# Feed-forward parts of a two-block kernel: own buffers for modulation blocks, the first two down blocks together, and three small preparations moved into steps

## Chip, cores and metric

One core of a Trainium2 chip runs the whole program. The metric is the time of one execution on the device in microseconds (us). The engines are TensorE (PE in the rows; PEld is its weight load), VectorE (DVE), ScalarE (ACT), GpSimd (POOL) and SyncE (SP), which here only issues transfers. TensorE has two clock levels, 1.2 and 2.4 GHz; a granted clock of 1.00 means the higher one throughout.

## What is computed

The reference chains two blocks over 256 tokens of width 1024. The first block has two layers of attention and feed-forward; the second takes the first's output, modulates it by values that come from a vector `c`, and runs two mixers and a mixture of small experts. Cut to what the change touches:

```python
for i in range(2):                                   # first block
    h = h + heads(rms_norm(h, norm_mix[i])) @ w_out[i]    # attention, i = 0 fox, i = 1 moba
    hn = rms_norm(h, norm_ffn[i])
    gu = hn @ w_gate_up[i]                           # 1024 -> 2 * 2816
    h = h + (silu(gu[..., :2816]) * gu[..., 2816:]) @ w_down[i]
x = rms_norm(h, norm_final)

mod = silu(c) @ w_ada + b_ada                        # second block, 1024 -> 6 * 1024
shift1, scale1, gate1, shift2, scale2, gate2 = split(mod, 6)
h = rms_norm_2(x, norm1_g) * (1 + scale1) + shift1
proj = h @ w_in                                      # latents, lru_x, lru_gate, merge logits
attn = mla_attention(...)                            # uses cos and sin of positions * inv_freq
rec = rg_lru_branch(...)                             # rates: softplus(-lru_lambda)
x = x + gate1 * (mix(attn, rec) @ w_out)
x = x + gate2 * peer_ffn(rms_norm_2(x, norm2_g) * (1 + scale2) + shift2, ...)
```

## The kernel before

All values are float32. A product is formed from three matmuls: each operand is split into a rounded part `hi` and the rest `lo`, and hi x hi, hi x lo and lo x hi are added in PSUM.

**The stream of weights.** A plan lists all weight blocks in the order in which they are used, each of 128 partitions by 1024 columns (512 KB). `Stream.load_to` (lines 183 to 193) issues their transfers on SP into one of four buffers `raw`; `split_to` makes `hi` on ScalarE (line 213) or, for a few blocks of the second block, on GpSimd (line 211), and `lo` on VectorE (line 214). There are four buffers for hi and three for lo, and blocks are split two ahead of use (`AHEAD`). The tile framework orders the instructions of every engine itself, by priority and by its own estimate of times; `issue_after` adds an edge to that order. An engine works off its list in that order.

**The feed-forward part of a layer** has 22 steps of 128 columns. Step f takes a gate and an up block (24 matmuls of 256 columns each, lines 350 to 353), then `gated` multiplies by the row scale `rb` (gu, line 681), applies Silu on ScalarE (684), forms the product (pr, 686) and splits it into `prh` (ScalarE, 338) and `prl` (VectorE, 339). The down block g (12 matmuls of 512 columns, lines 364 to 368) adds the product into four PSUM accumulators; `down_at` (line 58) puts it two steps (`LAG`) behind its gate block, so down 0 follows up block 2. In steps 8 to 15 of layer 0 `mem_chunk` prepares the second layer's memory (`mtl`, line 335).

**The modulation** has 48 blocks of `w_ada`, which are not split: `ada` (line 766) multiplies a block by Silu(c) and sums, in one VectorE instruction (line 774). They lie in the same plan and in the same four raw buffers: one at each feed-forward step of both layers, after that step's up block, and six more in the head projections of layer 1.

**Small preparations.** `csilu` (line 739) loads `c` and applies Silu in layer 0's heads. `prepare_second` (line 832) stands between out-projection and row statistics of layer 0: `angles` (Sin) and `lru_consts` (Abs, Exp and 39 small VectorE operations in both together). The row of the final norm, `gf2`, is loaded and squared at step 2 of layer 1 in program order (lines 707 to 710); the framework issues its load in layer 0's feed-forward part.

**Entry of the second block.** The first blocks of `w_in` (lx) run before the row scale `r` is known: `first_adaln` adds four sums of squares (`ss`) into `s4` on GpSimd (line 958), forms `r` there (lines 288 to 302), and after block lx3 the scale is spread over the partitions by TensorE (line 321). On GpSimd hi casts of lx1, lx4 and lx6 stand in the same list.

## Time and profile before

| | |
|---|---|
| median of 3 runs | 1707.04 us (1702.47 to 1709.91) |
| profiled execution | 1711.15 us, span 1709.3 us, mean granted clock 0.992 |
| TensorE busy in the span | 1675.5 us (98%) |
| VectorE busy | 1215.4 us (71%) |
| ScalarE busy | 875.3 us (51%) |
| GpSimd busy | 298.2 us (17%) |
| moved by transfers | 311.97 MB, 183 GB/s over the span |

The span is the part of the execution that the profile covers. Matmuls overlap each other, so a busy time of one matmul is longer than the distance between two starts. A row of a timeline gives the start in us from the span's start, the duration, the engine, the line in the kernel, the operation with out<-in and the tile's shape, and in brackets how long the engine was idle just before and whose work released it. A row of a table of windows gives, for a stretch, its length, each engine's busy time with the number of instructions, TensorE's granted clock, the busy share of the 16 DMA engines and the rate of the transfers.

### The profile page before, as it was taken

How to read it: one execution, taken by the hardware profiler on the slowest of the kernel's cores; microseconds unless marked ns; L12 is line 12 of the kernel's file. 1: busy time of each engine (PE TensorE's matmuls, PEld its weight loads, DVE VectorE, ACT ScalarE, POOL GpSimd, SP SyncE). 2: the span in 40 equal slices, each digit the busy share in tenths (PEclk: the TensorE clock that was granted, in tenths of full speed). 3: DMA queues.
4: the chain of work that ended last, by engine and by line, in shares of the span. 5: the costliest groups of instructions: out<-in, count | busy, mean ns of one | idle time of the engine just before them, and what ended most of it. 6: DMA issues, size and time to landing. Idle time of an engine off the chain costs nothing.

```text
span 1709.3 us, 30746 instructions
## 1 busy us (share of the span) xinstructions
PE 1675.5 (98%) x11724; PEld 1534.3 (90%) x11724; DVE 1215.4 (71%) x2418; ACT 875.3 (51%) x1500; POOL 298.2 (17%) x396
## 2 busy tenths in 40 slices
PE   8999999999999999999999999999999999999998
PEld 7878998998899998898999999999999888888887
DVE  5767676667676677868777979677888755555555
ACT  5555444455554444689464545444444444444443
POOL 5201000000110003210000010088888300000000
PEclk9999999999999999999999999999999999999999
DMA  6425767765377775453566565644444566666663
GB/s 202 159 87 187 243 231 238 244 210 177 100 242 241 243 240 164 163 185 112 161 209 185 174 184 174 203 145 147 141 144 145 176 186 187 192 187 188 189 188 126
DMA packets 86947, 311.97 MB, mean 183 GB/s; under 512 B 9744, under 2 KB 11024, under 8 KB 86288
## 3 DMA queue, kind: packets, MB, share of 16 engines
q1 hardware_dynamic: 86624, 308.96, 57.2%
q8 instruction: 93, 1.52, 0.4%
q10 hardware_dynamic: 144, 1.05, 0.2%
q14 instruction: 54, 0.44, 0.1%
q0 software_dynamic: 32, 0.00, 0.0%
HBM read 307.87 MB, written 2.10 MB: 181 GB/s over the span
## 4 chain that ended last, share of the span: by engine, by line
PE 52%; DVE 2%; ACT 2%; DMA 1%; issue 0%; POOL 0%; ACTq 0%; DVEq 0%; SPq 0%
PE pb L351 8%; PE pb L350 8%; PE pb L353 8%; PE pa L365 8%; PE pa L364 8%; PE pa L368 7%; PE pa L1543 3%; DVE lo L214 1%; PE pa L353 1%; PE pa L351 0%; PE pa L350 0%; PE pa L1444 0%; DMA raw<-in_w_mg_dram 0%; ACT QT L1149 0%; DMA raw<-in_w_query_dram 0%
## 5 line engine op out<-in xcount | busy, mean ns | idle before, releaser
L214 DVE TENSOR_TENSOR lo<-raw,hi 128x1024 fp32r<-128x1024 f32 (+1 forms) x532 | 649.1, 1221 | 314.0 <-PE pa L368 196.6
L213 ACT ACTIVATE hi<-raw 128x1024 fp32r<-128x1024 f32 (+2 forms) x517 | 541.5, 1050 | 606.6 <-PE pa L365 217.6
L350 PE MATMUL pb<-h1h,hi 128*128 128x256 f32 x1264 | 309.9, 285 | 3.6 <-POOL hi L211 3.0
L351 PE MATMUL pb<-h1l,hi 128*128 128x256 f32 x1264 | 303.8, 280 | 0.6 <-DVE h1l L923 0.6
L1542 POOL TENSOR_SCALAR ring<-iota,slots 128x128 f32<-128x128 f32 x256 | 207.2, 824 | 254.8 <-DVE slots L1509 135.4
L350 PEld LDWEIGHTS pb<-h1h,hi 128*128 128x128 f32 x1264 | 237.6, 188 | 5.1 <-POOL hi L211 3.2
L351 PEld LDWEIGHTS pb<-h1l,hi 128*128 128x128 f32 x1264 | 238.6, 189 | 1.2 <-DVE h1l L923 0.9
L350 PE MATMUL pb<-xth,hi 128*128 128x256 f32 (+1 forms) x936 | 229.4, 284 | 0.0
L351 PE MATMUL pb<-xtl,hi 128*128 128x256 f32 (+1 forms) x936 | 228.1, 282 | 0.0
L364 PE MATMUL pa<-hi,ring_v 128*128 128x512 f32 x512 | 201.9, 395 | 1.1 <-ACT ring_v L338 1.1
L365 PE MATMUL pa<-hi,ring_v 128*128 128x512 f32 x512 | 202.3, 396 | 0.0
L350 PEld LDWEIGHTS pb<-xth,hi 128*128 128x128 f32 (+1 forms) x936 | 178.1, 190 | 6.3 <-issue 2.8
L351 PEld LDWEIGHTS pb<-xtl,hi 128*128 128x128 f32 (+1 forms) x936 | 177.3, 189 | 2.6 <-issue 0.8
L353 PE MATMUL pb<-h1h,lo 128*128 128x256 f32 x1264 | 173.4, 279 | 0.0
L353 PEld LDWEIGHTS pb<-h1h,lo 128*128 128x128 f32 x1264 | 159.0, 188 | 0.0
L368 PE MATMUL pa<-lo,ring_v 128*128 128x512 f32 x512 | 141.1, 396 | 0.0
L353 PE MATMUL pb<-xth,lo 128*128 128x256 f32 (+1 forms) x936 | 129.0, 280 | 4.3 <-DVE lo L214 4.3
L353 PEld LDWEIGHTS pb<-xth,lo 128*128 128x128 f32 (+1 forms) x936 | 117.5, 187 | 5.6 <-DVE lo L214 5.3
L364 PEld LDWEIGHTS pa<-hi,ring_v 128*128 128x128 f32 x512 | 96.2, 188 | 24.3 <-ACT ring_v L338 1.4
L365 PEld LDWEIGHTS pa<-hi,ring_v 128*128 128x128 f32 x512 | 96.1, 188 | 23.6
L368 PEld LDWEIGHTS pa<-lo,ring_v 128*128 128x128 f32 x512 | 96.2, 188 | 23.3
L774 DVE CUSTOM_DVE_ANT_0 raw<-raw,r_rows 128x1024 f32<-128x1024 f32 x48 | 58.7, 1224 | 70.6 <-DMA raw<-in_w_ada_dram 70.5
(431 smaller groups left out, 2476.8 us busy)
## 6 DMA issues: line engine op xcount, KB each, us to landing
raw<-in_expert_u_dram SPq DMA_DIRECT2D x128, 512.0 KB, 3.7
raw<-in_expert_v_dram SPq DMA_DIRECT2D x128, 512.0 KB, 4.3
raw<-in_w_ada_dram SPq DMA_DIRECT2D x48, 512.0 KB, 4.6
raw<-in_w_gate_dram SPq DMA_DIRECT2D x44, 512.0 KB, 3.6
raw<-in_w_up_dram SPq DMA_DIRECT2D x44, 512.0 KB, 4.5
raw<-in_w_down_dram SPq DMA_DIRECT2D x44, 512.0 KB, 4.5
raw<-in_w_out_dram SPq DMA_DIRECT2D x24, 512.0 KB, 3.7
raw<-in_w_mg_dram SPq DMA_DIRECT2D x16, 512.0 KB, 3.4
```

The costliest lines, as they stand in the source:

```text
L213: first = nc.scalar.activation(hi[:, :w], raw[:, :w], AF.Copy)
L214: self.last = first, nc.vector.tensor_tensor(lo[:, :w], raw[:, :w], hi[:, :w], OP.subtract)
L350: mm(p, w[0][:, s], xt[0][:, kc, :], start=kc == 0, stop=False)
L351: mm(p, w[0][:, s], xt[1][:, kc, :], start=False, stop=False)
L353: mm(p, w[1][:, s], xt[0][:, kc, :], start=False, stop=kc == nk - 1)
L364: mm(p, xt[0][:, kc, ts], w[0][:, w0:w0 + n], start=start, stop=False)
L365: mm(p, xt[1][:, kc, ts], w[0][:, w0:w0 + n], start=False, stop=False)
L368: mm(p, xt[0][:, kc, ts], w[1][:, w0:w0 + n], start=False, stop=stop)
L774: nc.vector.tensor_tensor_reduce(out=w, in0=w, in1=self.csb, scale=1.0, scalar=0.0, op0=OP.mult, op1=OP.add, accum_out=self.mod[:, j:j + 1])
L1542: nc.gpsimd.tensor_scalar(ob, iota, slots[:, 1, t:t + 1], None, op0=OP.is_equal)
L1543: nc.tensor.matmul(p[:, j * 128:(j + 1) * 128], oa, ob, start=True, stop=True, skip_group_check=True)
```

## The change

The modulation blocks get two buffers of their own (`ada`), counted apart from the four raw buffers, and may be loaded further ahead in the plan. Downs 0 and 1 both stand at step 3. The pool of the feed-forward part's small tiles is gone; its tiles are slices of tiles under names that the attention part used, with four slots for a product instead of three. `csilu` becomes `load_c`, and its Silu stands after the squares of the row statistics; in layer 1 a Silu of one column stands there. `angles` stands at step 4 of layer 0, `lru_consts` at step 6; the load of `gf2` at step 6 of layer 1 and its Square at step 9. The core of the diff:

```diff
+ADA_BUFS = 2
 def down_at(f):
-    return [NF - 3, NF - 2, NF - 1] if f == NF else [] if f < LAG or f - LAG > NF - 4 else [f - LAG]
+    if f == NF:
+        return [NF - 3, NF - 2, NF - 1]
+    return [0, 1] if f == LAG + 1 else [f - LAG] if LAG + 1 < f < NF - 3 + LAG else []
...
+    def is_ada(self, j):
+        return self.plan[j][0][0] == "ada"
     def load_to(self, n):
...
-            if self.raw and j - min(self.raw) >= RAW_BUFS:
+            ada = self.is_ada(j)
+            if sum(self.is_ada(k) == ada for k in self.raw) >= (ADA_BUFS if ada else RAW_BUFS):
                 return
...
-            t = self.raw_pool.tile([128, 1024], F32, tag="raw", name="raw")
+            if ada:
+                t = self.ada_pool.tile([128, 1024], F32, tag="ada", name="ada")
+            else:
+                t = self.raw_pool.tile([128, 1024], F32, tag="raw", name="raw")
...
-            self.load_to(self.n_split + RAW_BUFS)
+            self.load_to(self.n_split + RAW_BUFS + ADA_BUFS)
...
-                                                   scalar=0.0, op0=OP.add, op1=OP.min, accum_out=mn[:, tt:tt + 1])
+                                                   scalar=3e38, op0=OP.add, op1=OP.min, accum_out=mn[:, tt:tt + 1])
...
-            self.ffn = ctx.enter_context(tc.tile_pool(name="ffn", bufs=2))
+            self.st.ada_pool = ctx.enter_context(tc.tile_pool(name="ada", bufs=ADA_BUFS))
...
-                            self.csilu()
+                            self.load_c()
...
-        dve = los[-1]
-        if i == 0:
-            with self.tc.issue_after(dve.ins), self.tc.issue_after(self.last_hi.ins):
-                self.prepare_second()
         r = self.row_stats()
+        with self.tc.issue_after(self.last_sq.ins):
+            if i == 0:
+                nc.scalar.activation(self.csb, self.csb, AF.Silu)
+            else:
+                warm = self.small.tile([128, 1], F32, tag="warm", name="warm")
+                nc.scalar.activation(warm, self.half[:, 0:1], AF.Silu)
...
+        gus = lay.tile([128, 2, 2, T], F32, tag="qT", name="gus")
+        sgs = lay.tile([128, 4, T], F32, tag="kT", name="sgs")
+        prs = lay.tile([128, 8, 1, T], F32R, tag="hdh", name="prs")
         def gated(f, p):
-            gu = self.ffn.tile([128, 2, T], F32, tag="gu", name="gu")
+            gu = gus[:, f % 2]
...
-            prods[f] = (self.ffn.tile([128, 1, T], F32R, tag="prh", name="prh", bufs=3),
-                        self.ffn.tile([128, 1, T], F32R, tag="prl", name="prl", bufs=3))
+            prods[f] = prs[:, f % 4], prs[:, 4 + f % 4]
...
-            if i and f == 2:
-                self.gf2 = self.load_rows(self.hx, "rows", D, tag="h1h", start=D)
-                nc.scalar.activation(self.gf2, self.gf2, AF.Square)
+            if i and f == 6:
+                with self.tc.issue_after(st.dma.ins):
+                    self.gf2 = self.load_rows(self.hx, "rows", D, tag="h1h", start=D)
+            if i and f == 9:
+                with self.tc.issue_after(st.last[0].ins):
+                    nc.scalar.activation(self.gf2, self.gf2, AF.Square)
+            if i == 0 and f in (4, 6):
+                with self.tc.issue_after(st.last[0].ins), self.tc.issue_after(st.last[1].ins):
+                    self.angles() if f == 4 else self.lru_consts()
```

What this does to the order of instructions is seen at three places. The first is SP's list of transfers at the start of layer 0's feed-forward part (`in_w_gate`, `in_w_up`, `in_w_down` and `in_w_ada` are the four kinds of blocks). Before:

```order
L191 DMA raw<-in_w_gate_dram 128x1024
L191 DMA raw<-in_w_up_dram 128x1024
L191 DMA raw<-in_w_ada_dram 128x1024
L191 DMA raw<-in_w_gate_dram 128x1024
L191 DMA raw<-in_w_up_dram 128x1024
L191 DMA raw<-in_w_ada_dram 128x1024
L191 DMA raw<-in_w_gate_dram 128x1024
L191 DMA raw<-in_w_up_dram 128x1024
L191 DMA raw<-in_w_ada_dram 128x1024
L191 DMA raw<-in_w_down_dram 128x1024
L191 DMA raw<-in_w_gate_dram 128x1024
L191 DMA raw<-in_w_up_dram 128x1024
```

Now:

```order
L201 DMA raw<-in_w_gate_dram 128x1024
L201 DMA raw<-in_w_up_dram 128x1024
L201 DMA raw<-in_w_gate_dram 128x1024
L201 DMA raw<-in_w_up_dram 128x1024
L201 DMA raw<-in_w_gate_dram 128x1024
L201 DMA raw<-in_w_up_dram 128x1024
L201 DMA raw<-in_w_gate_dram 128x1024
L201 DMA raw<-in_w_up_dram 128x1024
L201 DMA ada<-in_w_ada_dram 128x1024
L201 DMA raw<-in_w_down_dram 128x1024 x2
L201 DMA ada<-in_w_ada_dram 128x1024
L201 DMA raw<-in_w_gate_dram 128x1024
```

The ada loads are gone from between the first four gate and up blocks, the first down block is loaded together with the second, one gate and up pair later, and the ada loads come closer together behind that: over the next ten steps there are two or three in a step, where there was one. All 48 are loaded by layer 1's value projection, two of them at the start of the program between its fourth and fifth value block (`in_w_v`); before, the last ones came at layer 1's step 18.

The second place is VectorE's list in the middle of layer 0's feed-forward part, one step from one gu to about the next (line 774 before, 794 after, is the ada product, in two rows; 214 and 224 the lo of a weight block; 335 and 345 the memory's lo). Before:

```order
L681 TENSOR_TENSOR gu<-pb,rb 128x512
L214 TENSOR_TENSOR lo<-raw,hi 128x1024
L686 TENSOR_TENSOR pr<-sg,gu 128x256
L335 SCALAR_TENSOR_TENSOR mtl<-pb,cols,mth 128x256
L214 TENSOR_TENSOR lo<-raw,hi 128x1024
L339 TENSOR_TENSOR prl<-pr,prh 128x256
L774 ISA raw,mod<-raw,r_rows 128x1024
L774 ISA mod 128x1
L214 TENSOR_TENSOR lo<-raw,hi 128x1024
L681 TENSOR_TENSOR gu<-pb,rb 128x512
```

Now:

```order
L698 TENSOR_TENSOR gus<-pb,rb 128x512
L224 TENSOR_TENSOR lo<-raw,hi 128x1024
L702 TENSOR_TENSOR sgs<-sgs,gus 128x256
L345 SCALAR_TENSOR_TENSOR mtl<-pb,cols,mth 128x256
L794 ISA ada,mod<-ada,r_rows 128x1024
L794 ISA mod 128x1
L349 TENSOR_TENSOR prs<-sgs,prs 128x256
L224 TENSOR_TENSOR lo<-raw,hi 128x1024
L794 ISA ada,mod<-ada,r_rows 128x1024
L794 ISA mod 128x1
L224 TENSOR_TENSOR lo<-raw,hi 128x1024
L794 ISA ada,mod<-ada,r_rows 128x1024
```

In the place of one ada product there are three in this step; between the gu of step 3 and that of step 13 there are 25 of them, where there were 10, beside 31 lo.

The third place is GpSimd's list at the entry of the second block (lines 211 and 221 are hi casts of w_in blocks, 958 and 975 the first operation of the chain that makes `r`, and the three rows behind are its next). Before:

```order
L1050 MEMSET r_rows_qk 128x2x32
L1051 TENSOR_SCALAR r_rows_qk<-r_rows_qk 128x96
L211 CAST hi<-raw 128x1024
L958 TENSOR_TENSOR s_7650<-ss_7589 128x4
L960 TENSOR_SCALAR mb<-s_7650 128x2
L961 TENSOR_SCALAR s_7650<-s_7650 128x2
L288 TENSOR_SCALAR ms<-s_7650 128x2
```

Now:

```order
L1067 MEMSET r_rows_qk 128x2x32
L1068 TENSOR_SCALAR r_rows_qk<-r_rows_qk 128x96
L221 CAST hi<-raw 128x1024 x2
L975 TENSOR_TENSOR s_7438<-ss_7377 128x4
L977 TENSOR_SCALAR mb<-s_7438 128x2
L978 TENSOR_SCALAR s_7438<-s_7438 128x2
L298 TENSOR_SCALAR ms<-s_7438 128x2
```

The cast of block lx6 has moved from behind the chain to ahead of it, and follows that of lx4 at once.

TensorE's own list changes little: down 0 and down 1 stand after up block 3 in both layers, where down 0 stood after up block 2, and the second block's order is as before.

## Rows read from the trace of the kernel before

**Rows 1.** The page: busy time, share and instructions of each engine.
```profile
PE 1675.5 (98%) x11724; PEld 1534.3 (90%) x11724; DVE 1215.4 (71%) x2418; ACT 875.3 (51%) x1500; POOL 298.2 (17%) x396
```

**Rows 2.** Windows (length, busy per engine, clock, DMA share, GB/s), layer 0's feed-forward part.
```profile
core 0: us, PE busy (x) PEld busy (x) DVE busy (x) ACT busy (x) POOL busy (x), PEclk, DMA share, GB/s
168.00:176.00 8.00, 6.76 (x32) 5.51 (x33) 6.80 (x19) 4.21 (x8) 0.00 (x0) 0.79 0.42 133
296.00:304.00 8.00, 6.25 (x36) 6.13 (x37) 5.33 (x8) 3.97 (x6) 0.00 (x0) 0.79 0.73 231
200.00:284.00 84.00, 83.98 (x605) 78.60 (x604) 58.40 (x82) 39.52 (x55) 0.00 (x0) 1.00 0.71 240
```

**Rows 3.** Timeline of TensorE: waits in both feed-forward parts, and two starts of downs.
```profile
168.95 0.65 PE L364 MATMUL pa<-hi,prh 128*128 128x512 f32 x1 [2.57 <-ACT prh L338]
...
297.75 1.21 PE L353 MATMUL pb<-xth,lo 128*128 128x256 f32 x8 [2.10 <-DVE lo L214]
...
303.15 0.39 PE L364 MATMUL pa<-hi,prh 128*128 128x512 f32 x1
...
311.54 0.39 PE L364 MATMUL pa<-hi,prh 128*128 128x512 f32 x1
...
317.36 1.20 PE L353 MATMUL pb<-xth,lo 128*128 128x256 f32 x8 [1.01 <-DVE lo L214]
...
494.30 0.97 PE L364 MATMUL pa<-hi,prh 128*128 128x512 f32 x3 [1.50 <-ACT prh L338]
...
626.51 1.20 PE L353 MATMUL pb<-xth,lo 128*128 128x256 f32 x8 [1.14 <-DVE lo L214]
```

**Rows 4.** Timeline of SP's queue and of ScalarE: the final norm's row.
```profile
287.37 0.38 SPq L248 DMA_DIRECT2D r_rows<-in_rows_dram  x1
...
294.06 1.06 ACT L710 ACTIVATE r_rows<-r_rows 128x1024 f32<-128x1024 f32 x1 [3.30 <-DMA r_rows<-in_rows_dram]
```

**Rows 5.** Timeline of VectorE: a small operation, one step, and later ada products.
```profile
170.16 0.16 DVE L883 TENSOR_SCALAR l_s<-l_s 128x8 f32<-128x8 f32 x1
...
284.51 1.23 DVE L774 CUSTOM_DVE_ANT_0 raw<-raw,r_rows 128x1024 f32<-128x1024 f32 x1 [2.02 <-DMA raw<-in_w_ada_dram]
...
285.66 1.22 DVE L214 TENSOR_TENSOR lo<-raw,hi 128x1024 fp32r<-128x1024 f32 x1
286.80 0.68 DVE L681 TENSOR_TENSOR gu<-pb,rb 128x512 f32<-128x512 f32 x1
...
288.53 0.42 DVE L686 TENSOR_TENSOR pr<-sg,gu 128x256 f32<-128x256 f32 x1
288.87 0.48 DVE L335 SCALAR_TENSOR_TENSOR mtl<-pb,cols,mth 128x256 fp32r<-128x256 f32 x1
289.26 1.22 DVE L214 TENSOR_TENSOR lo<-raw,hi 128x1024 fp32r<-128x1024 f32 x1
...
295.33 1.22 DVE L774 CUSTOM_DVE_ANT_0 raw<-raw,r_rows 128x1024 f32<-128x1024 f32 x1 [4.11 <-DMA raw<-in_w_ada_dram]
...
314.93 1.23 DVE L774 CUSTOM_DVE_ANT_0 raw<-raw,r_rows 128x1024 f32<-128x1024 f32 x1 [3.59 <-DMA raw<-in_w_ada_dram]
```

**Rows 6.** Windows, same columns: the two densest longer stretches of transfers.
```profile
3.50:11.50 8.00, 4.16 (x21) 3.62 (x20) 4.56 (x7) 4.61 (x9) 7.86 (x6) 0.83 0.99 332
...
482.00:492.00 10.00, 10.00 (x88) 10.00 (x87) 8.35 (x11) 4.56 (x5) 2.41 (x5) 1.00 0.87 314
```

**Rows 7.** Issues of transfers, 176 to 340 us: count, KB each, median us to landing.
```profile
raw<-in_w_ada_dram SPq DMA_DIRECT2D x18, 512.0 KB, 4.7
```

**Rows 8.** Timeline of ScalarE: a table load.
```profile
165.63 1.28 ACT L684 ACT_TABLE_LOAD   x1
```

**Rows 9.** Timeline of GpSimd at the second block's entry.
```profile
671.66 1.04 POOL L211 CAST hi<-raw 128x1024 fp32r<-128x1024 f32 x1 [8.72 <-PE pa L351]
673.33 1.11 POOL L958 TENSOR_TENSOR s<-ss 128x4 f32<-128x4 f32 x1 [0.64 <-DVE ss L954]
```

**Rows 10.** Timeline of TensorE there: block lx2's lo pass, the spread of r.
```profile
674.74 1.13 PE L353 MATMUL pa<-x1h,lo 128*128 128x258 f32 x8
...
679.85 0.43 PE L321 MATMUL pb<-ident,r 128*128 128x128 f32 x2 [1.10 <-POOL r L302]
```

More of the change, by code (lines that the diff above doesn't have):

```diff
@@ L174, in __init__ @@
         self.split_pool = ctx.enter_context(tc.tile_pool(name="wsplit", bufs=LO_BUFS))
-        self.last = ()
+        self.last, self.ada_pool = (), None
         self.n_loaded = self.n_split = self.n_taken = 0
@@ L280, in sumsq @@
     def sumsq(self, src, dst, junk):
-        self.nc.scalar.activation(junk, src, AF.Square, accum_out=dst)
+        return self.nc.scalar.activation(junk, src, AF.Square, accum_out=dst)
     def rstd(self, ss, n, w):
@@ L531, in row_stats @@
             for tt in range(2):
-                self.sumsq(self.h[:, tt, :], ss[:, tt:tt + 1], self.junk)
+                self.last_sq = self.sumsq(self.h[:, tt, :], ss[:, tt:tt + 1], self.junk)
         return self.rstd(ss, D, 2)
@@ L669, in layer @@
                       lambda kc: los.append(self.norm_chunk(xt2, kc, self.g_ffn, i)), lambda: finish(0))
[L670 to L673 removed]
         r = self.row_stats()
+        with self.tc.issue_after(self.last_sq.ins):
[4 more added lines that the diff above has]
+                nc.scalar.activation(warm, self.half[:, 0:1], AF.Silu)
         acc = [[self.psA(), self.psA()] for _ in range(2)]
         prods = {}
+        gus = lay.tile([128, 2, 2, T], F32, tag="qT", name="gus")
+        sgs = lay.tile([128, 4, T], F32, tag="kT", name="sgs")
+        prs = lay.tile([128, 8, 1, T], F32R, tag="hdh", name="prs")
         def gated(f, p):
[L680 removed]
+            gu = gus[:, f % 2]
             nc.vector.tensor_tensor(gu, p.rearrange("p (a t) -> p a t", a=2),
                                     rb[:, None, :].to_broadcast([128, 2, T]), OP.mult)
[L683 removed]
+            sg, pr = sgs[:, f % 2], sgs[:, 2 + f % 2]
             nc.scalar.activation(sg, gu[:, 0, :], AF.Silu)
[L685 removed]
             nc.vector.tensor_tensor(pr, sg, gu[:, 1, :], OP.mult)
[L687 to L688 removed]
+            prods[f] = prs[:, f % 4], prs[:, 4 + f % 4]
             self.split((prods[f][0][:, 0, :], prods[f][1][:, 0, :]), pr)
@@ L737, in layer, with load_c @@
         return xt
-    def csilu(self):
+    def load_c(self):
         self.csb = self.load_rows(self.hx, "rows", D, tag="h1l")
-        self.nc.scalar.activation(self.csb, self.csb, AF.Silu)
     def out_proj(self, key, x, order, evict, after, between=None):
@@ L830, in gate_rows @@
             self.nc.vector.tensor_copy(t[:, k * 512:(k + 1) * 512], p)
-    def prepare_second(self):
-        self.angles()
-        self.lru_consts()
     def angles(self):
```

2 lines of the change are left out of this document (removed).

## Prediction

> **What bounds the kernel now.** I read the page first, then the windows, then TensorE's timeline at its waits, then the other engines around each wait. The page names TensorE: busy 1675.5 of 1709.3 us, VectorE 1215.4, ScalarE 875.3 [rows 1]. So only what leaves TensorE waiting, or slows its clock, is worth anything. The windows sort the stretches [rows 2]: from 200 to 284 us, ten steps of layer 0's feed-forward, TensorE is busy for 83.98 of 84 us at the full clock (2.4 GHz), while VectorE has 25.6 us and ScalarE 44 us free. A step there takes 311.54 - 303.15 = 8.39 us from one down block to the next [rows 3]. This stretch cannot get shorter; it can only get longer. What can get shorter are the holes at its edges. TensorE waits 2.57 us for the first down block's product (ScalarE's prh), 2.10 and 1.01 us for a lo half late in layer 0, 1.50 us for layer 1's first product, and 1.14 us for a lo half at the end of layer 1's feed-forward [rows 3]. After the two longest, the granted clock is 0.79 on average over 8 us [rows 2]: part of the stretch ran at 1.2 GHz, which costs 8 x 0.21 = 1.7 us each time.
>
> **The sum's base.** The rows come from one execution of 1711.15 us (span 1709.3, 1.85 around it). The median of the three runs is 4.1 us lower. I sum against 1711.15 and then take off 4.1.
>
> **Removed: waits.**
> (a) Layer 0's first down block. Today it stands after the third up block, and prh comes 2.57 us late. Moved one step, downs 0 and 1 stand after the fourth up block: two blocks of 24 matmuls, 5.6 us (the step less its twelve wide matmuls, 8.39 - 2.8), lie in between, more than the 2.57 us. Products 0 and 1 now have to live longer, which their four slots allow. Gain 2.6 + 1.7 = 4.3.
> (d) Likewise layer 1's first down block: 1.5. It had no visible drop of the clock behind it.
> (b) The wait at 297.75. The final norm's row is issued on SP at 287.37, ahead of an ada load, lands 6.7 us later, and its Square on ScalarE starts at 294.06 after 3.30 us of waiting [rows 4]. All hi casts stand behind that Square; at the same time VectorE waits 4.11 us for the ada block [rows 5]. The change puts load and Square into steps 6 and 9 of layer 1. Gain 2.1 + 1.7 = 3.8. In its new place ScalarE has the 6.7 us of landing covered by three steps of 8.39, so I cost it at nothing; without that cover it would be 3.3 again.
> (c) The lo waits at 317.36 and 626.51 come behind an ada product that itself waits for its load (3.59 us of VectorE idle ahead of the first) [rows 5]. In the changed order no ada stands at either place. Gain 1.0 + 1.1 = 2.1.
> Sum of the gains: 11.7. It cannot be more than these holes hold, since nothing in the change shortens matmuls.
>
> **Added: (f) the dense stretch.** The ada blocks no longer take their turn in the four raw buffers, one per step. Their two own buffers let the planner load them ahead: 25 stand between the gated products of steps 3 and 13, not 10. VectorE's bill for these ten steps, by pitch on its timeline [rows 5]: 25 ada and 31 lo at 1.15 us (284.51 to 285.66) 64.4; ten each of gu 0.68, pr 0.34 and prl taken as pr, 13.6; five mtl at 0.39, 2.0; 39 small operations of angles and rates at about 0.1, 3.9. Together 83.9 of the 84 us that ten steps take. So VectorE, with 30% free today, has nothing left for waits, and it executes in order: an ada product that waits for its load holds up the lo behind it, and TensorE needs that. The transfers: 55 blocks of 0.524 MB, 28.8 MB in 84 us, or 343 GB/s. Today's stretch has 240 [rows 2]. The densest stretches of the trace are 332 GB/s over 8 us at the start, with the engines 0.99 busy, and 314 over 10 us in layer 1 [rows 6]. At 320 GB/s, 28.8 MB take 90 us: +6. Bounds: zero, if the queue holds 343 when it is kept full; +18, from the loop of the two ada buffers. That loop is landing 4.7 us [rows 7], product 1.15, turn-round some 0.9: 6.8 us for two blocks, so 25 take 85 us, just level; with a landing of 6 us, nearer to the 6.7 of [rows 4], they take 100, +16, and 2 more for the clock. I take +6, since today's landings of 4.7 us are from a stretch at 70% of that load.
> The Trainium skill, "DMA: Bandwidth & Descriptors", section Specifications, gives about 358 GB/s of HBM bandwidth for each NeuronCore. By it 28.8 MB would take 80 us, the DMA would not bound this stretch, and the sum would be 6 us less. No window of 8 us or more in this trace comes to that figure.
>
> **Moved, at little or nothing.** Angles and rates leave the place before the row statistics, from where their small operations on VectorE reach in among the first gated products (170.16) [rows 5]; their 3.9 us are in (f). On ScalarE the change has 23 table loads for 24, of 1.28 us [rows 8]; two now lie in steps 6 and 7, behind 44 us of free time over ten steps, so nothing; uncovered they would be 2.6. The new start of the min reduction changes no duration.
> (h) Start: two ada loads (1.05 MB) go between the fourth and fifth value block, while the queue is 0.99 busy [rows 6]. At 332 GB/s they are 3.2 us of transfer, mostly behind matmuls that run until then: +0.5, bounds 0 to 3.
> (i) The five last ada loads stand between layer 1's value loads: +0.5, bounds 0 to 4.
>
> **(g) Entry of the second block.** On POOL the cast for block lx6 now stands ahead of the chain that makes r. Today that chain starts at 673.33, right behind lx4's cast at 671.66 [rows 9]. The cast for lx6 needs the hi buffer of block lx2, which TensorE gives back when its hi pass ends, at 674.74 [rows 10]: cast from 674.9 to 675.95, chain some 2.6 us later. TensorE waits 1.10 us for r now [rows 10], so it would wait 3.7, which is longer than the waits that were followed by half clock; with 1.7 for that it makes +4 (bounds 0, if the cast finds its buffer early, and +7).
>
> **Sum:** -11.7 + 6 + 4 + 0.5 + 0.5 = -0.7: 1710.4 against 1711.15; 4.1 lower, **1706 us**. What the holes give, the dense stretch and the entry take back.
>
> **Rivals.**
> (B) The dense stretch is covered. Transfers hold 343 GB/s, ada blocks sit in their buffers before VectorE comes, and the loss in (f) is 0 to 3; the entry costs 2. For it: a queue with more issues waiting is fuller, and landing covers turn-round. Against it: no window shows that rate for long. Time: -11.7 + 2 + 2 + 1 is -7, down to -12: 1695 to 1700, middle 1697. The page's bandwidth figure above would make this the case.
> (C) Slower: the ada loop. When two blocks take longer than 6.7 us from load to load (2.5 blocks in 8.39 us), each ada product makes VectorE wait, the lo halves queue behind it, and TensorE stands at each. The deciding point is a landing of about 4.7 us in the stretch. At 6 us it is +16, with the clock +18: 1706 + 12 = 1718, and up to 1722 with the entry's upper bound. For it: VectorE waits at ada products already now, up to 4.11 us [rows 5], with landings at 4.7; the r_rows load took 6.7. Against it: these waits are today's late issue behind other raw buffers, which the own buffers end.
> (D) The change does not end the first wait: three ada products now stand ahead of the row scale rb, the third waits for its load, and products 0 and 1 come that much later. (a) is lost: about 1710.
>
> **How the numbers follow.** 0.5%, 8.5 us, is about what a measurement of this kernel can tell from no change: 1698.5 to 1715.6. Forecast (between -8 and +8) 0.50; B 0.27, nearly all beyond -8.5 if (f) is nothing; C 0.18; D 0.05, some of it slower if the waits add up. Faster 0.28, same 0.50, slower 0.22. The range goes from all gains at the lowest costs, 1695, less 2 for the spread of the runs, to C's 1718 and 1 more: 1693 to 1719. The likeliest case alone: 1699 to 1713.
>
> **What would show it.** (a), (b), (c), (d) right: no TensorE idle over 1 us before the first down block of either layer, and none behind an ada product at the end of layers 0 and 1. (f) right: VectorE 95% busy between steps 3 and 13, transfers at 320 GB/s, and ten steps in 90 us, with TensorE's idle released by lo; at 84 us B holds, at 100 us with VectorE waiting for ada loads C holds. (g) right: TensorE's wait for r at the entry at 3 to 4 us with a lower clock behind it. The prediction is wrong if the dense stretch costs under 2 or over 12 us.

## Result and profile after

The changed kernel takes 1719.36 us (median of 6 runs, 1716.38 to 1721.59), the kernel before 1707.21 in the same set: a ratio of 1.0072, 95% interval 1.0056 to 1.0088. It is slower by 12 us, where 1706 us and no change had been forecast, and it lies just above the forecast range of 1693 to 1719 us.

The page of the changed kernel has the same matmuls and almost the same work on every engine; TensorE is busy 9 us longer than in [rows 1].

```profile
PE 1684.8 (98%) x11724; PEld 1542.4 (90%) x11724; DVE 1220.1 (71%) x2418; ACT 875.9 (51%) x1500; POOL 291.6 (17%) x396
```

Since TensorE's order is nearly the same, the same matmul can be found in two traces, and the difference of its two starts says where time is gained or lost. This table gives by how many us that difference grew in each stretch (limits in the time of the kernel before; every trace is set against the profiled execution of the kernel before, which ended 4 us above its median). The lower rows belong to experiments told below.

| kernel | to 102 | 102-127 | 127-202 | 202-285 | 285-327 | 327-654 | 654-690 | 690-815 | 815-1353 | sum |
|---|---|---|---|---|---|---|---|---|---|---|
| changed | -1.3 | +1.8 | -4.4 | +7.8 | -4.9 | -3.4 | +4.9 | +4.3 | +5.5 | +10.3 |
| before_shift | -1.1 | 0.0 | -0.8 | +0.5 | -1.2 | -1.7 | +0.3 | +1.2 | +6.3 | +3.4 |
| before_shift64 | -2.3 | 0.0 | +0.2 | +1.1 | -3.3 | +0.4 | +0.1 | +2.1 | +9.1 | +8.5 (1.2 behind 1353) |
| before_shift256 | -2.2 | 0.0 | +1.1 | -0.3 | 0.0 | -0.9 | +0.1 | +0.6 | +0.1 | -1.6 |
| after_noshift | -1.3 | +1.8 | -4.8 | +2.8 | -5.4 | -2.0 | +5.6 | -0.4 | +0.1 | -3.7 |
| after_held | -1.9 | +1.9 | -4.2 | +0.5 | -4.9 | -3.1 | +6.2 | -1.2 | +5.3 | -1.3 |
| after_sums | -1.5 | +3.4 | -4.3 | +4.7 | -4.9 | -0.6 | +1.4 | +4.8 | +6.2 | +9.1 |
| noshift_first_downs | -1.0 | +1.8 | -4.1 | +5.4 | -5.3 | -1.3 | +5.5 | +4.6 | -1.0 | +4.5 |
| held_noshift | -1.7 | +1.8 | -4.8 | -0.3 | -5.3 | -3.7 | +6.1 | -1.6 | -1.6 | -10.9 |
| held_noshift_sums | -0.2 | +1.8 | -4.8 | -0.3 | -5.3 | -4.5 | +1.4 | +0.2 | -0.1 | -11.9 |
| repaired_shared | -1.4 | +1.8 | -4.8 | +3.2 | -3.5 | +0.1 | +1.4 | +0.1 | -1.3 | -4.4 |
| repaired_all_three_back | -1.4 | 0.0 | -3.8 | -0.3 | -5.3 | -4.2 | +1.4 | +0.5 | -0.2 | -13.4 |
| three_back_shared | -1.6 | 0.0 | -3.3 | +2.7 | -4.0 | +3.7 | +1.5 | +0.3 | -0.8 | -1.6 |

The three before_shift kernels have the kernel before's order of instructions. What they gain or lose in a stretch whose work is the same shows how far two executions differ: about 2 us at the start and 3 us around 300. So the traces say where, and the times how much. Their waits differ too: ahead of layer 0's first down block TensorE waits 2.52, 1.86 and 3.33 us in them (2.57 in the kernel before), for the lo behind the final norm's row 2.07, 0.60 and 3.04 us (2.10 before), and the waits of 1.01 and 1.14 us that the forecast counted as (c) occur in none of them at these lengths.

The forecast gains are all there: 127-202 (first down block), 285-327 (final norm's row) and part of 327-654. What outweighs them stands in four places, and there is a smaller one in layer 0's attention (102-127).

**Layer 0's dense stretch.** Windows of the changed kernel, columns as in [rows 2]; the first runs from the gu of step 3 to that of step 13:

```profile
174.74:272.45 97.71, 95.27 (x668) 87.94 (x666) 83.67 (x155) 45.25 (x64) 0.00 (x0) 1.00 0.88 309
200.00:284.00 84.00, 79.53 (x546) 72.91 (x545) 70.62 (x129) 38.56 (x53) 0.00 (x0) 0.98 0.87 301
...
270.00:284.00 14.00, 11.97 (x76) 10.87 (x76) 11.55 (x19) 7.25 (x11) 0.00 (x0) 0.88 0.72 246
```

Where TensorE was busy 83.98 of 84 us (200 to 284), it now has 79.53, and the clock falls behind the longest wait. The timelines of TensorE (all its waits in this stretch) and of VectorE (two of its long waits at an ada product):

```profile
209.18 1.21 PE L363 MATMUL pb<-xth,lo 128*128 128x256 f32 x8 [0.73 <-DVE lo L224]
...
244.31 1.21 PE L363 MATMUL pb<-xth,lo 128*128 128x256 f32 x8 [0.48 <-DVE lo L224]
...
254.33 1.21 PE L363 MATMUL pb<-xth,lo 128*128 128x256 f32 x8 [0.71 <-DVE lo L224]
...
260.90 1.22 PE L363 MATMUL pb<-xth,lo 128*128 128x256 f32 x8 [0.47 <-DVE lo L224]
...
274.71 1.21 PE L363 MATMUL pb<-xth,lo 128*128 128x256 f32 x8 [2.02 <-DVE lo L224]
```

```profile
241.29 1.22 DVE L794 CUSTOM_DVE_ANT_0 ada<-ada,r_rows 128x1024 f32<-128x1024 f32 x1 [2.24 <-DMA ada<-in_w_ada_dram]
...
271.30 1.23 DVE L794 CUSTOM_DVE_ANT_0 ada<-ada,r_rows 128x1024 f32<-128x1024 f32 x1 [4.25 <-DMA ada<-in_w_ada_dram]
```

The lo that TensorE waits for at 274.71 stands on VectorE behind the ada product that waited 4.25 us until 271.30. The chain of the forecast is there, 4.4 us of it as waits. The loads issued from 260.9 to 267.2, around the longest wait, took 6.4 to 7.3 us to land; the median over the whole stretch is 4.9. The size varies from one execution to the next: the three other traces with products crowded like this (after_noshift, after_sums, noshift_first_downs) lost 2.8, 4.7 and 5.4 us here, and not 7.8.

**Entry of the second block.** Timelines of TensorE, GpSimd and VectorE, and as the last VectorE's last sum in the kernel before:

```profile
679.11 0.69 PE L331 MATMUL pb<-ident,r 128*128 128x128 f32 x2 [4.81 <-POOL r L312]
```

```profile
670.60 1.07 POOL L221 CAST hi<-raw 128x1024 fp32r<-128x1024 f32 x1 [2.97 <-PE pa L361]
673.44 1.11 POOL L975 TENSOR_TENSOR s<-ss 128x4 f32<-128x4 f32 x1 [1.77 <-DVE ss L971]
```

```profile
672.67 0.68 DVE L971 CUSTOM_DVE_ANT_0 junk<-sq,r_rows 128x512 f32<-128x512 f32 x1
```

```profile
671.73 1.51 DVE L954 CUSTOM_DVE_ANT_0 junk<-sq,r_rows 128x512 f32<-128x512 f32 x1 [0.37 <-ACT sq L282]
```

TensorE waits 4.81 us for r, not 1.10 as in [rows 10]. But the cast of lx6 ended at 671.67; GpSimd then waited 1.77 us more for the last of the four sums, which VectorE made from 672.67 to 673.35. The chain starts as late in absolute time as in [rows 9], although all before it had come 4 us earlier. The cause, tested below, is VectorE's order: before, the framework had put the first sum (662.55) and the second (667.12) among the splits of the token chunks, and now all four stand behind them, the first at 666.68. From 680 to 690 us the granted clock is 0.90, where it was 1.00.

**Matmuls that are each a little slower.** From 815 to 1353 us TensorE waits no longer than before (it is busy for 535.96 of these 538 us, and was for 534.94), its clock is 1.00 in both kernels, and yet 5.5 us go. The window from 1110 to 1310 us, in the kernel before and in the changed one:

```profile
1110.00:1310.00 200.00, 200.00 (x1736) 200.00 (x1735) 166.15 (x410) 90.24 (x211) 175.99 (x216) 1.00 0.48 145
```

```profile
1110.00:1310.00 200.00, 200.00 (x1714) 200.00 (x1713) 160.49 (x391) 89.39 (x205) 167.68 (x205) 1.00 0.47 144
```

In 200 us TensorE gets through 1714 matmuls instead of 1736, 1.3% fewer. By the distance from one start to the next, the median over the same rows, the matmuls that read h1l (the lo half of the transposed tokens) take 119 ns and not 117.

**A wait at 787.78** of 2.47 us for VectorE, which with the lower clock behind it (0.77 from 785 to 800) makes most of the 4.3 us in 690-815. VectorE was late because a row of the final norm, issued at 765.78, arrived at 772.49:

```profile
787.78 2.07 PE L393 MATMUL pa<-QT,QT 96*128 96x128 f32 x6 [2.47 <-DVE mn L409]
```

The column 690-815 shows such a loss in some executions and not in others of the same order (-0.4 in after_noshift), so the order alone does not bring it. Three of the four traces with crowded products have it, and of the other changed kernels repaired_gf2 (+4.6) and in part held_noshift_sums_csilu (+2.5); whether the crowding makes it more frequent is not shown.

### The profile page after: what moved, and what is told of

Same layout as the page of the kernel before. It is cut to its first block, busy times and chain, and to the rows that moved or that the text cites. A ratio compares the mean times of both kernels' runs of the same rounds, so it can differ in the third digit from the quotient of the medians.

```text
span 1719.6 us, 30784 instructions
## 1 busy us (share of the span) xinstructions
PE 1684.8 (98%) x11724; PEld 1542.4 (90%) x11724; DVE 1220.1 (71%) x2418; ACT 875.9 (51%) x1500; POOL 291.6 (17%) x396
## 4 chain that ended last, share of the span: by engine, by line
PE 53%; DVE 3%; DMA 1%; ACT 1%; issue 0%; POOL 0%; DVEq 0%; ACTq 0%; SPq 0%
PE pb L360 8%; PE pb L361 8%; PE pb L363 8%; PE pa L375 8%; PE pa L378 7%; PE pa L374 7%; PE pa L1560 3%; DVE lo L224 1%; PE pa L363 1%; PE pa L361 0%; PE pa L360 0%; PE pa L1461 0%; DMA r_rows<-in_rows_dram 0%; DMA raw<-in_w_query_dram 0%; DVE rr L1334 0%
## 5 line engine op out<-in xcount | busy, mean ns | idle before, releaser
L360 PE MATMUL pb<-h1h,hi 128*128 128x256 f32 x1264 | 314.0, 287 | 2.6 <-POOL hi L221 2.0
L361 PE MATMUL pb<-h1l,hi 128*128 128x256 f32 x1264 | 307.9, 282 | 0.8 <-DVE h1l L940 0.8
L794 DVE CUSTOM_DVE_ANT_0 ada<-ada,r_rows 128x1024 f32<-128x1024 f32 x48 | 58.6, 1222 | 30.0 <-DMA ada<-in_w_ada_dram 28.8
```

The lines of the kernel that those rows point to most:

```text
L360: mm(p, w[0][:, s], xt[0][:, kc, :], start=kc == 0, stop=False)
L361: mm(p, w[0][:, s], xt[1][:, kc, :], start=False, stop=False)
L794: nc.vector.tensor_tensor_reduce(out=w, in0=w, in1=self.csb, scale=1.0, scalar=0.0, op0=OP.mult, op1=OP.add, accum_out=self.mod[:, j:j + 1])
```

## Experiments

Ratios are to the kernel before, timed in the same set of runs.

**The position of the tiles.** The one-column Silu of layer 1 got a tile of its own, `warm`, with four slots of 32 bytes in the pool of small tiles. All tiles allocated behind it (token rows, transposed tokens, the experts' tiles) lie 128 bytes higher in each partition; the weights' buffers do not move. *before_shift* puts an unused tile there in the kernel before:

```diff
         r = self.row_stats()
+        if i:
+            self.small.tile([128, 1], F32, tag="warm", name="warm")
```

> The kernel before, with one unused column tile of four slots in the pool of small tiles: its 128 bytes per partition push every later tile (token rows, transposed tokens, the experts' tiles) up by 128 bytes, as the change's one-column Silu tile does. The order of instructions is the same on all engines. Theory 1 (the position of the tiles makes the matmuls slower): matmuls between 880 and 1350 us stretch by 0.15 to 0.35 us in 20 us and in layer 1's feed-forward part by 0.15, 6 us in all: 1713. Theory 2 (that stretching belongs to the one profiled execution or to something else in the change): no difference, 1707 within 2.

Measured: 1715.76 against 1704.72, 1.0058 (1.0035 to 1.0081). *after_noshift* takes the tile out of the change:

```diff
-                warm = self.small.tile([128, 1], F32, tag="warm", name="warm")
-                nc.scalar.activation(warm, self.half[:, 0:1], AF.Silu)
+                warm = self.small.tile([128, 2], F32, tag="inv", name="inv")
+                nc.scalar.activation(warm[:, 0:1], self.half[:, 0:1], AF.Silu)
```

> The changed kernel with the one-column Silu writing into an existing slot of the small tiles (tag inv) and not into a tile of its own, so that all later tiles lie where they lay before the change; the order of instructions is the same. Theory 1: the 6 us of slow stretching go, 1713. Theory 2: no difference, 1719 within 2.

Measured: 1709.12, 1.0025 (1.0013 to 1.0037). Both agree with theory 1, with more than its 6 us, and exclude theory 2: the same order of instructions, and 128 bytes cost some 10 us in the one kernel and 8 us (1.0072 less 1.0025, of 1707) in the other. The matmuls account for it: over all that start within 0.3 us of the one before them in both traces, the distances between starts add up to 10.0 us more in before_shift than in the kernel before (8.9 of them behind 500 us, 6.4 between 815 and 1353), and to 9.1 us more in the changed kernel than in after_noshift. The window of 1110 to 1310 us, before_shift, then after_noshift:

```profile
1110.00:1310.00 200.00, 200.00 (x1713) 200.00 (x1713) 163.20 (x401) 89.73 (x209) 173.27 (x213) 1.00 0.46 143
```

```profile
1110.00:1310.00 200.00, 200.00 (x1735) 200.00 (x1734) 166.45 (x411) 90.16 (x212) 176.40 (x217) 1.00 0.47 144
```

*before_shift256* and *before_shift64* are the same edit with 256 and 64 bytes:

```diff
+            self.small.tile([128, 16], F32, tag="warm", name="warm")
...
+            self.small.tile([128, 1], F32, tag="warm", name="warm", bufs=2)
```

> The kernel before with the later tiles pushed up by 256 bytes and not 128; same order of instructions. If the matmuls' extra time depends on where a tile lies within 256 bytes, it is gone: 1705, and matmuls that read h1l take 116.0 ns on average between 1110 and 1310 us. If any place other than the old one is slow, or if the slowness has a longer period: 1710 to 1716 and 118 to 119 ns.

Measured: 1707.23 against 1705.35, 1.0014 (1.0000 to 1.0029): the loss is gone, or nearly.

> The kernel before with the later tiles pushed up by 64 bytes; same order of instructions. Where the tile of transposed tokens begins, modulo 256, is 64 in the kernel before (fast), 192 with 128 bytes (slow) and 64 with 256 bytes (fast); here it is 128. If only what lies 128 off is slow: 1705. If any start other than 64 is slow: 1710 to 1716, with matmuls that read h1l at 118 to 119 ns and not at 116.

Measured: 1720.92 against 1705.45, 1.0083 (1.0066 to 1.0099): 64 bytes cost most, more than the 1716 expected at the highest; the median distance at h1l is 123 ns. The same window, 256 bytes, then 64:

```profile
1110.00:1310.00 200.00, 200.00 (x1735) 200.00 (x1734) 166.54 (x412) 89.83 (x210) 176.54 (x218) 1.00 0.46 143
```

```profile
1110.00:1310.00 200.00, 200.00 (x1701) 200.00 (x1701) 161.66 (x395) 89.01 (x206) 170.21 (x209) 1.00 0.46 143
```

**The crowding of modulation products.** *after_held*:

```diff
-            self.ada(1, f == 0)
+            self.ada(1, True)
```

> The changed kernel with each modulation product held behind its step's lo split, one per step as before, still in two buffers of its own. Theory of the ada loop: the 7.8 us that layer 0's steps 3 to 13 lost against the kernel before go, with the gains at the first downs kept: 1711 to 1712, ten steps in 84 us. Rival (what slowed these steps is the rate of transfers or the two small preparations, not the crowding of ada products): at most 3 us are gained, 1716 or more.

Measured: 1711.98, 1.0053 (1.0036 to 1.0070). The stretch 202-285 loses 0.5 us instead of 7.8. Its window, and its ada loads (number, KB, median us to landing):

```profile
200.00:284.00 84.00, 84.00 (x596) 78.52 (x595) 64.77 (x114) 43.24 (x59) 0.00 (x0) 1.00 0.77 245
```

```profile
ada<-in_w_ada_dram SPq DMA_DIRECT2D x10, 512.0 KB, 4.5
```

TensorE is busy throughout, with the same two buffers: in this stretch it is the crowding that costs. The whole time gains less than the stretch: the kernel before was 2.5 us faster in this set, and 1.0072 less 1.0053 is 0.19% or 3 us, within the intervals and at the limit of what the rival allowed. Without the shift the gain is clear: held_noshift (below) has 0.9975 where after_noshift has 1.0025, 0.50% or 8.5 us. Between these two traces the dense stretch gives 3.1 us of 7.2; the rest is spread over the columns behind 327.

**The order of the sums.** *after_sums* writes the loop of the sums into the loop over the halves, so that VectorE's list has the first two sums ahead of the second half's splits:

```diff
             late()
-        for nh in range(2):
-            c = slice(nh * 512, (nh + 1) * 512)
             for tt in range(2):
                 k = 2 * tt + nh
```

> The changed kernel with the sums of squares at the second block's entry written behind each half of the chunks and not behind both, so that on VectorE the first two sums come before the second half's splits and GpSimd's chain for r stands before the cast of lx6. Theory (TensorE's wait for r at the entry, some 5 us with the clock, is the order of these sums): 1714. Rival (the chain starts when TensorE gets there, whatever the order): 1719 within 2.

Measured: 1715.71, 1.0060 (1.0043 to 1.0078). The stretch 654-690 loses 1.4 us and not 4.9. The time alone, 0.12% less than the changed kernel's and within the intervals, does not settle it. *held_noshift* leaves only this repair out of the kernel with all three:

> The kernel with two of the three repairs: one product per step and no shift, the sums in the order of the change. Theory: the entry of the second block is 4 us longer than in the kernel with three repairs (5.5 against 1.5 us lost there), so 1701. Rival (the entry's wait is hidden in most executions): 1698 or less.

Measured: 1700.23, 0.9975 (0.9962 to 0.9989), 654-690 at +6.1. *held_noshift_sums* has all three repairs:

> The changed kernel with three repairs at once: one modulation product per step, the one-column Silu in an existing slot (no shift), and the sums of squares behind each half. If the three losses are separate and add (5 for the crowding, 8 for the shift, 3 to 4 for the sums, from 1717 on the chip that gave 1704.7 for the kernel before): 1700, which is 0.2 to 0.4% faster than the kernel before. Rival (they share a wait, or something else of the change costs as much): 1705 or more.

Measured: 1696.98 against 1705.35, 0.9951 (0.9935 to 0.9966). The sums are worth 0.24%, 4 us, and the repaired change is faster than the kernel before by 0.5%. Whether the three losses add is not shown: all repairs together gain 1.21% (21 us) over the changed kernel, each alone 0.47, 0.19 and 0.12% (13 us in all), and the intervals are too wide to tell these apart. Nor was the kernel before run with its sums in the new order; but the repaired kernel still loses 1.4 us against it in 654-690, so its gain does not lie there. TensorE and GpSimd at the entry, in held_noshift_sums:

```profile
667.81 0.43 PE L331 MATMUL pb<-ident,r 128*128 128x128 f32 x2 [1.09 <-POOL r L312]
```

```profile
661.89 0.20 POOL L973 TENSOR_TENSOR s<-ss 128x4 f32<-128x4 f32 x1 [1.77 <-DVE ss L969]
...
668.10 1.04 POOL L221 CAST hi<-raw 128x1024 fp32r<-128x1024 f32 x1
```

The wait for r is back at its old length, 1.09 us.

**Which part brought which gain.** *noshift_first_downs* is after_noshift with the old `down_at`:

```diff
-    return [0, 1] if f == LAG + 1 else [f - LAG] if LAG + 1 < f < NF - 3 + LAG else []
+    return [] if f < LAG or f - LAG > NF - 4 else [f - LAG]
```

> The changed kernel without the shift (1709.1), and with the first two down blocks again at steps 2 and 3. Theory: TensorE's waits ahead of the first down block return in both layers with their lower clock, 4.3 and 1.5 us: 1715. Rival (the product is in time anyway in the new order of VectorE): 1709 within 2.

Measured: 1707.59, 1.0022 (1.0004 to 1.0041), not slower than after_noshift; TensorE waits 0.39 us at layer 0's first down block and not at all at layer 1's. A miss of the theory. From here on one part is put back into held_noshift_sums. *repaired_downs* (old `down_at`):

> The kernel with three repairs, and the first two down blocks again at steps 2 and 3. From the earlier run with the old place: a wait of at most 0.5 us in layer 0 and none in layer 1, so 1697 to 1697.7. Rival (with one ada product per step VectorE's order brings the wait back): 1699 to 1701.

Measured: 1698.23, 0.9966 (0.9954 to 0.9978). *repaired_prep*:

```diff
+        if i == 0:
+            with self.tc.issue_after(los[-1].ins), self.tc.issue_after(self.last_hi.ins):
+                self.angles()
+                self.lru_consts()
         r = self.row_stats()
...
-            if i == 0 and f in (4, 6):
-                with self.tc.issue_after(st.last[0].ins), self.tc.issue_after(st.last[1].ins):
-                    self.angles() if f == 4 else self.lru_consts()
```

> The kernel with three repairs (1697.0), and angles and rates again before layer 0's row statistics. The run with the old place of the first downs still had no wait there, so another part must have removed it. Theory: it was these preparations, whose small VectorE operations stood among the first gated products: TensorE again waits about 2.5 us for the first down block of layer 0, with the clock 4.5 us: 1701. Rival (two causes, each enough: the later downs cover what the preparations delay): no wait over 0.5 us, 1697.

Measured: 1697.23, 0.9958 (0.9945 to 0.9972), no wait at the first down block. *repaired_gf2*:

```diff
-            if i and f == 6:
-                with self.tc.issue_after(st.dma.ins):
-                    self.gf2 = self.load_rows(self.hx, "rows", D, tag="h1h", start=D)
-            if i and f == 9:
-                with self.tc.issue_after(st.last[0].ins):
-                    nc.scalar.activation(self.gf2, self.gf2, AF.Square)
+            if i and f == 2:
+                self.gf2 = self.load_rows(self.hx, "rows", D, tag="h1h", start=D)
+                nc.scalar.activation(self.gf2, self.gf2, AF.Square)
```

> The kernel with three repairs, and the final norm's row loaded and squared at step 2 of layer 1 in program order, which puts both into layer 0's feed-forward part again (order differs in these two instructions alone). Theory: TensorE's wait of 2.1 us for a lo half behind ScalarE's wait for this row comes back, with the clock 3.8 to 4.4 us: 1701. Rival (that wait came from the ada load behind it on SP, which own buffers have taken away): 1697 within 1.5.

Measured: 1698.21, 0.9964 (0.9952 to 0.9976). The rival: 285-327 keeps its whole gain, -5.3, though ScalarE's Square waits 3.18 us for the row, about as long as in [rows 4]. *repaired_shared* (the modulation blocks in the raw buffers again):

```diff
-            if sum(self.is_ada(k) == ada for k in self.raw) >= (ADA_BUFS if ada else RAW_BUFS):
+            if self.raw and j - min(self.raw) >= RAW_BUFS:
...
-            if ada:
-                t = self.ada_pool.tile([128, 1024], F32, tag="ada", name="ada")
-            else:
-                t = self.raw_pool.tile([128, 1024], F32, tag="raw", name="raw")
+            t = self.raw_pool.tile([128, 1024], F32, tag="raw", name="raw")
...
-            self.load_to(self.n_split + RAW_BUFS + ADA_BUFS)
+            self.load_to(self.n_split + RAW_BUFS)
```

> The kernel with three repairs, but with the modulation blocks in the four raw buffers again. Theory (own buffers bring something: an ada load no longer stands ahead of the gate and up loads for the same buffers, and the lo waits of 1.0 and 1.1 us late in layer 0 and at the end of layer 1 go): these waits come back, 1699 to 1700. Rival (held to one per step, own buffers are worth nothing): 1697 within 1.

Measured: 1705.71, 1.0011 (0.9998 to 1.0024). The theory held in kind, with a larger size: held to one product per step, own buffers are worth 0.6% of 1707, 10 us (0.45 to 0.53% against the three kernels of its own set), 3.5 of them in the stretch 202-285 of the trace and 4.6 in 327-654. But the two named waits did not come back: TensorE now waits for hi casts, 1.10 us at 218.81, 0.86 at 290.50 and 1.96 at 335.40. The 2.10 us for a lo half stay away too, with the row moved and without own buffers. *held_noshift_sums_csilu*:

```diff
                             self.load_c()
+                            nc.scalar.activation(self.csb, self.csb, AF.Silu)
...
-            if i == 0:
-                nc.scalar.activation(self.csb, self.csb, AF.Silu)
-            else:
+            if i:
```

> The three repairs, and Silu of c again right behind its load in layer 0's heads, as before the change. All traces of the changed kernel show layer 0's attention between 105 and 120 us 1.8 to 2 us longer than before. If the place of this Silu (its tables, and with it ScalarE's order there) is the cause, that stretch gets 1.8 us shorter and the run as much against the kernel with three repairs; and the first gated product of layer 0 may pay a table load again. Rival (the order there comes from the two early modulation loads): the stretch stays as long.

Measured: 1696.27, 0.9951 (0.9936 to 0.9966). The stretch 102-127 loses nothing now instead of 1.8 us, in this trace and in the three others with that Silu in the heads; the time shows no difference from held_noshift_sums. It is the lowest median of all in us, but not clear of its neighbours.

The wait ahead of the first down block took four more runs, all on held_noshift_sums. *repaired_prep_downs* (the edits of repaired_prep and repaired_downs):

> The kernel with three repairs, with angles and rates again before the row statistics and the first two downs again at steps 2 and 3. Each alone brought no wait back. If these two are the causes, each enough: TensorE waits 2 to 3 us for layer 0's first down block, 1700 to 1701. If it is the Silu table, which stands ahead of the first gated product only where Silu of c is not behind the squares: no wait over 0.5 us, 1698.

Measured: 1699.62, 0.9968 (0.9953 to 0.9984), no wait. *repaired_csilu_downs* (those of held_noshift_sums_csilu and repaired_downs):

> The kernel with three repairs, Silu of c in layer 0's heads again (so the Silu table is loaded right ahead of the first gated product) and the first two downs again at steps 2 and 3; angles and rates stay inside the steps. If the table load alone makes the first product late: a wait of about 1.3 us or more ahead of the first down block. If it takes the preparations: none over 0.5 us.

Measured: 1697.62, 0.9951 (0.9932 to 0.9969), a wait of 0.31 us. *repaired_all_three_back* (all three, and no one-column Silu):

> The kernel with three repairs, and all three back: downs at steps 2 and 3, angles and rates before the row statistics, Silu of c in the heads and none behind the squares in either layer. Every theory of this wait expects it here: 2 to 3 us ahead of layer 0's first down block, 1.5 us ahead of layer 1's; 1702. If it is absent, the wait belonged to the ada loads in the raw buffers or to the old slots of the products.

Measured: 1697.76, 0.9944 (0.9925 to 0.9963), no wait. So none of the three. What is left first are own buffers, and ScalarE's timeline says how. The cast ahead of the Silu, in the kernel before and in repaired_all_three_back:

```profile
164.55 1.06 ACT L213 ACTIVATE hi<-raw 128x1024 fp32r<-128x1024 f32 x1 [1.57 <-DMA raw<-in_w_gate_dram]
```

```profile
161.60 1.06 ACT L221 ACTIVATE hi<-raw 128x1024 fp32r<-128x1024 f32 x1 [2.32 <-PE pb L359]
162.68 1.28 ACT L698 ACT_TABLE_LOAD   x1
163.97 0.42 ACT L698 ACTIVATE sgs<-gus 128x256 f32<-128x256 f32 x1
```

Before, the first Silu (166.93) stood behind a cast that waited for a gate block, whose load SP issued at 158.56, behind those of a modulation block (155.96) and a down block (157.25). With own buffers that block is there, and the Silu runs 3 us earlier, table load and all; 1.4 of them are this execution's head start (column to 102). *three_back_shared* adds the edit of repaired_shared:

> The run with all three parts back, and with the modulation blocks in the four raw buffers again. In the trace of the kernel before, ScalarE's Silu for the first product stands behind a hi cast that waits for a gate block until 164.55 us, and that load waits for a buffer behind two modulation blocks. Theory (own buffers alone end the wait, moved downs alone too): here neither is there, so TensorE waits 2 to 3 us ahead of layer 0's first down block, and the run takes 1705 to 1708. Rival (one product per step or the new slots of the products ended it): no wait over 0.5 us.

Measured: 1703.04, 0.9982 (0.9969 to 0.9994); waits of 0.77 and 0.20 us at layer 0's first down block, less than expected. At layer 1's the wait is back in full: 1.85 us for prh (here `prs`, L342) and 0.56 for prl, where repaired_all_three_back has none and the kernel before 1.50 [rows 3]. TensorE, then ScalarE:

```profile
489.60 0.73 PE L368 MATMUL pa<-hi,prs 128*128 128x512 f32 x2 [1.85 <-ACT prs L342]
```

```profile
488.19 1.06 ACT L217 ACTIVATE hi<-raw 128x1024 fp32r<-128x1024 f32 x1 [1.68 <-DMA raw<-in_w_gate_dram]
489.15 0.71 ACT L342 ACTIVATE prs<-sgs 128x256 fp32r<-128x256 f32 x2
```

A cast that waits for a gate block stands ahead of the product's cast. So a late gate block in front of ScalarE does bring this wait, and the buffers alone end it: nothing else differs between these two kernels. With own buffers the wait stays away whichever part is put back; in shared buffers it stays away with the other parts of the change in place (repaired_shared, -4.8), so those parts together are enough too; which of them is not shown. In layer 0, with neither, 1.0 us came back and not 2.5, and the gate block was not late there. What made up the rest in the kernel before stays open.

## Why the prediction was wrong

By its own steps:

- **What failed: "nothing in the change shortens matmuls", taken for "changes", and the part "moved, at little or nothing".** The one-column Silu was looked at for its table load alone. Its tile moved everything behind it by 128 bytes, and matmuls, most of them behind 500 us, became up to 1.3% slower: 8 us, shown by two pairs of kernels with the same order of instructions. No term and no rival had it. Without it the result is 1.0025, 4 us slower, inside the range and on the side of no change; the 5 us that still separate it from the forecast's 1 us faster are not traced to one place.
- **(a), (d), first downs: right in size, wrong in cause.** Forecast 4.3 and 1.5; the stretch 127-202 gained 4.4 to 4.8. But with the old place of the downs the gain stayed: with own buffers the move has nothing left to gain. The row named the releaser (prh), and I stopped there; the Silu behind a cast behind a late gate block was two steps further back on ScalarE. The 1.7 us for the clock are not sure either: behind the wait of 2.52 us in before_shift the granted clock stays at 1.00 from 160 to 182 us.
- **(b), (c): right in size for one execution, wrong in part of the cause.** Forecast 3.8 and 1.0 in this stretch; 4.9 to 5.4 came, against an execution that had both waits. With the row's load back at its old step the gain came all the same, so with own buffers the move is not needed; with the move and shared buffers 3.5 us of it stayed (repaired_shared). The waits of (c) are not in the three other traces with the order before, so its 2.1 us are largely a matter of that one execution.
- **(f), the dense stretch: about right in size, by luck; wrong in mechanism.** Forecast +6 from the rate of transfers; four traces show +2.8 to +7.8. VectorE's bill was right, 83.67 us busy against 83.9, but it is not a full engine: the ten steps take 97.71 us, where those steps took 88.89 before, so that it is 86% busy and not 95%. The transfers run at 309 GB/s and not 320. What costs is waits in order: loads that take 4.9 us at the median, and 6.4 to 7.3 around the longest wait, behind an issue that waits for a buffer. This is rival C's mechanism at the forecast's price. In C's loop the turn-round of 0.9 us came from no row: in the changed kernel SP issues the next ada load 0.03 us after 30 of 38 products of layer 0's steps and 1.5 to 2.5 us after the others, and the 25 loads of these ten steps land after 5.4 us at the median, not 4.7.
- **(g), the entry: right in place and in size, wrong in cause.** Forecast +4, measured 4. GpSimd's order had changed as said, but the cast of lx6 held nothing up; what the chain waited for was the last sum on VectorE, whose order the forecast did not look at.
- **(h), (i):** nothing that can be told from the spread of executions. **Not in the sum:** Silu of c behind the squares, 1.8 us of layer 0's attention in the trace.
- **Rivals.** C gave 1718, near the result by luck: it had a dense stretch of +18, and got less than half of that. B's time did not come, and only one of the four traces has a dense stretch within its 0 to 3. D's mechanism did not occur.

On the rate of transfers: over 84 us the changed kernel shows 301 GB/s at a DMA share of 0.87. The figure of the Trainium skill that the prediction names, about 358 GB/s ("DMA: Bandwidth & Descriptors", section Specifications), was not reached in any such stretch here. But it is no ceiling in this case: at its start the changed kernel moves 393 GB/s over 8 us, and the measurement decides.

```profile
8.00:16.00 8.00, 6.15 (x30) 5.44 (x31) 7.20 (x10) 4.15 (x8) 7.84 (x4) 0.79 1.01 393
```

So neither 320 nor 358 GB/s was the limit of the dense stretch; as far as the traces tell, VectorE's order and the two buffers held the loads back.

## What to carry to other kernels

Look at where a change puts its tiles as well as at what it orders: one column with a few slots, allocated early in a pool, moved every later tile, and cost more than any wait in the sum. Own buffers for a side stream were worth 10 us when its consumer was also held to its step; left free, the planner crowded an engine that executes in order, and gave back 8.5. A wait in one trace is not yet a wait of the kernel: of the holes that the sum counted, two were missing in the next three executions of the same order. When a row names who released a wait, follow that engine's list back until the step at which something is late by itself, before a moved instruction gets the credit.

## What the runs showed of the hardware

The rate of fp32 matmuls with 256 columns depends on where in the partition their tiles begin. With the same order of instructions and the weights in their old place, moving all tiles allocated behind them by 0, 64, 128 and 256 bytes (h1l then begins 64, 128, 192 and 64 bytes behind a multiple of 256) gave ratios of 1, 1.0083, 1.0058 and 1.0014, and 1736, 1701, 1713 and 1735 matmuls in 200 us, at a granted clock of 1.00 each. With 256 bytes the old rate is back, or nearly; four places do not show more of a period. Which of the moved tiles does it, and whether a place faster than the old one exists, was not tried. The other surprise is the landing of one 512 KB load of a single row spread over the partitions: from 4.6 us (issued 761.93, used at 766.52 in after_noshift) to 6.7 us (765.78 to 772.49 in the changed kernel) at the same place of the program; with the first TensorE does not wait for VectorE there, with the second 2.47 us.
